# Loading layer 1's modulation weights four tiles at a time, from buffers of their own

## The chip, the cores and the metric

The kernel runs on one core of one Trainium2 chip. The metric is device time in microseconds (us) of one execution, and 2509.45 us is the median of three before the change.

## What is computed

One step of a two-layer model runs over 128 context tokens and 1024 latent tokens, each 1024 wide. Layer 0 mixes tokens by a state-space recurrence, layer 1 by windowed pooling, and each layer then has a gated feed-forward part of width 2816. In each layer six vectors, the modulation, are made from one conditioning vector per kind of token, and they shift, scale and gate everything else:

```python
def ada_mod(cond, w, b):
    m = (jax.nn.silu(cond) @ w + b)[..., None, :]
    return jnp.split(m, 6, axis=-1)

for i in range(DEPTH):
    sh1c, sc1c, g1c, sh2c, sc2c, g2c = ada_mod(c_ctx, ada_w[i], ada_b[i])
    sh1l, sc1l, g1l, sh2l, sc2l, g2l = ada_mod(c, ada_w[i], ada_b[i])
    hc, hl = modulate(xc, sh1c, sc1c), modulate(xl, sh1l, sc1l)
    ...
    xl = layer_norm(DEEPNORM_ALPHA * xl + g1l * ol, ln_g[i, 0], ln_b[i, 0])
    fl = swiglu(modulate(xl, sh2l, sc2l), ffn_w_gate[i], ffn_w_up[i], ffn_w_down[i])
    xl = layer_norm(DEEPNORM_ALPHA * xl + g2l * fl, ln_g[i, 1], ln_b[i, 1])
```

`ada_w` is 2 x 1024 x 6144 numbers of 4 bytes, so layer 1's half is 25 MB. None of layer 1's modulation is needed before layer 1 begins.

## The kernel before, in words

**The modulation in steps.** A layer's modulation is made in three banks of two vectors each. `ada_steps(l, b)` is a generator for one bank: 16 steps, each of which loads one 512 KB tile `adaw` of `ada_w` over SyncE's DMA queue (SP) and multiplies it by the conditioning (`cond`, 32 columns of which two are used) in four matmuls, one for each 32-column strip of TensorE, into one PSUM tile `ada`. In the text these four matmuls are a *group*, and groups that stand next to each other on TensorE are a *run*. After the last group the bank is finished: ScalarE copies the tile to `arow`, four small DMAs on ScalarE's queue scatter it into the 32 rows of `ar`, TensorE transposes `ar` into `adat`, and VectorE adds the bias into `mod` and derives gates (`vecs`). Before the change all of this is in the last step.

**Where the steps are taken.** `ada_rest` strings five banks together: layer 0's second and third, which are stepped in the state-space part (`ssm`), and layer 1's three. Layer 1's are taken as a filler in layer 0's feed-forward part (`build`): one step after each pass of three loops. The latent tokens are two blocks A and B of 512. `ffn_up(A)` has 22 passes, each with a gate tile and an up tile of weights and 48 matmuls `ffn` of 128x128 by 128x512. `ffn_down(A)` has 2 x 11 passes with one weight tile and 24 matmuls `dn`. `ffn_up(B)` follows, and its first four passes take the last four steps. In this stage only, `adaw` and `arow` come from the pool `raw`, three buffers of 512 KB that also take every weight tile.

**How a weight tile gets to TensorE.** SP loads it into `raw`. ScalarE rounds it to `wh`, VectorE makes the rest `wl` (`split_into`, L776 and L777), three buffers each, and TensorE multiplies `wh` twice and `wl` once (L792 to L794). The inputs of `ffn_down` are split in the same way into `hkh` and `hkl`.

**What sets the order.** Every engine and every DMA queue runs its instructions in the order in which they stand. A scheduler puts them there when the program is built, from a simulated timeline, so the order of the code is not the order on an engine.

Of the kernel before, what the change touches and what calls it, by code (L numbers as in the profile page):

```python
# [11 lines left out]
F32 = mybir.dt.float32  # L12
F32R = mybir.dt.float32r
I32 = mybir.dt.int32
AF = mybir.ActivationFunctionType
# [26 lines left out]
class Kernel:  # L42
# [88 lines left out]
    def ada_steps(self, l, b, pool=None):  # L131

        nc, I = self.nc, self.I
        def ring(n, name):
            q = pool or self.adp
            if q is None:
                return self.raw.tile([128, n], F32, tag="raw", name=name)
            return q.tile([128, n], F32, tag="ad", name=name, bufs=4 if pool else 2)

        tag = "s" if self.adp else "c"  # L140
        ps = self.psum(f"ada{l}{b}", tag)
        for hf in range(2):
            for k in range(8):
                w = ring(1024, f"adaw{l}{b}{k}{hf}")
                c0 = b * 2048 + hf * 1024
                nc.sync.dma_start(w, I["ada_w"][l, k * 128:(k + 1) * 128, c0:c0 + 1024])
                for cg in range(4):
                    nc.tensor.matmul(ps[32 * cg:32 * cg + 32, 256 * hf:256 * hf + 256], self.cond[:, k, :],
                                     w[:, cg * 256:(cg + 1) * 256], start=(k == 0), stop=(k == 7))
                if (k, hf) != (7, 1):  # L150
                    yield None
        arow = (self.raw.tile([128, 512], F32, tag="raw", name=f"arow{l}{b}") if pool
                else ring(512, f"arow{l}{b}"))
        nc.scalar.activation(arow, ps, AF.Copy)
        ar = self.sm.tile([32, 128], F32, tag="ar", name=f"ar{l}{b}", bufs=1)
        for i in range(2):
            for v in range(2):
                nc.scalar.dma_start(ar[16 * i + 8 * v:16 * i + 8 * v + 8, :], arow[i:128:32, 256 * v:256 * v + 256])
        pt = self.psum(f"adat{l}{b}", tag)
        nc.tensor.transpose(pt[:, 0:32], ar, self.ident[:32, :32])  # L160
        nc.vector.tensor_tensor(
            self.mod[l][:, 2 * b:2 * b + 2, :, :].rearrange("p v i k -> p i v k"),
            pt[:, 0:32].rearrange("p (i v k) -> p i v k", i=2, v=2),
            self.adab[:, l * 48 + b * 16:l * 48 + b * 16 + 16]
            .rearrange("p (v k) -> p v k", v=2).unsqueeze(1).to_broadcast([128, 2, 2, 8]), op=OP.add)
        self.vecs(l, b)
        yield arow

    def ada_bank(self, l, b, pool=None):
        for r in self.ada_steps(l, b, pool):  # L170
# [1 line left out]
        return r  # L172

    def ada_rest(self):
        for l, b in ((0, 1), (0, 2), (1, 0), (1, 1), (1, 2)):
            yield from self.ada_steps(l, b)


    def ssm_params(self, pool, tmp, ad):
# [459 lines left out]
    def ssm(self):  # L639
        self.adp = self.rawc = None  # L640
        R = self.side
        right, left = ExitStack(), ExitStack()
        pright = self.pright
        self.sk = left.enter_context(R("ssk", "left"))
        pp = right.enter_context(R("ssp"))
        so = right.enter_context(R("sso"))
        si = right.enter_context(R("ssi"))
        with R("sst") as tmp:
            with R("ad0", "left") as ad:
                arow = self.ssm_params(pp, tmp, ad)  # L650
            self.ssm_modvec(pp, tmp, arow)
            self.ssm_dskip(pp, tmp)
        self.u = left.enter_context(R("ssmu", "left")).tile([128, G, NCH], F32, name="u")
        self.adp = self.rawc = None
        self.Z = []
        self.late = []
        self.ada = fill = self.ada_rest()
        with R("ssu") as tmp, R("sse") as early:
            for kt in range(KT):
                self.ssm_u(tmp, kt)  # L660
                if kt == 0:
                    self.ssm_u_ctx(tmp)
                    self.Z.append(left.enter_context(R("ssmz0", "left")).tile([128, 145, 64], F32, name="Z0"))
                self.step(fill, 1)
                self.ssm_in(si, 0, kt, early, 14)
                self.ssm_tables(so, kt, si)
            while self.late:
                self.ssm_v()
        self.Z.append(left.enter_context(R("ssmz1", "left")).tile([128, 145, 64], F32, name="Z1"))
        for kt in range(KT):  # L670
            self.ssm_in(si, 1, kt, si, 3)
            self.step(fill, 1)
        while self.late:
            self.ssm_v()
        self.ssm_scan_ctx(si)
        right.close()
        pright.close()
        for t, b in (("s", 1), ("a", 5)):
            self.pp[t] = self.st.enter_context(self.tc.tile_pool(name="psx" + t, bufs=b, space=PSUM, side="right"))
        cblk = right.enter_context(R("cblk"))  # L680
        self.open_ctx(cblk)
        self.open_hc(cblk)
        with R("ssy") as tmp:
            self.adp = tmp
            self.yb = [tmp.tile([128, 8, 8, 16], F32, tag="yl", name=f"yb{q}", bufs=2) for q in range(2)]
            self.yct = [tmp.tile([128, 128], F32, name=f"yct{x}") for x in range(2)]
            for q in range(2):
                self.nc.gpsimd.memset(self.yb[q], 0.0)
                self.nc.gpsimd.memset(self.yct[q], 0.0)
            for kt in range(KT):  # L690
                self.ssm_y_ctx(tmp, kt)
                self.step(fill, 2)
            self.ctx0a()
            self.ssm_scan_lat()
            self.adp = self.rawc = None
            for kt in range(KT):
                self.ssm_y(tmp, kt)
        left.close()
        self.cright = right
# [374 lines left out]
    def build(self):  # L1074
        tc, nc = self.tc, self.nc
        with ExitStack() as st:
# [19 lines left out]
            fill = self.ctx0b()  # L1096
# [5 lines left out]
            A, B = [Block(512, 0, self.X[q], True, "a", tl, "") for q in range(2)]  # L1102
            halves = lambda b: [Block(256, 0, b.x[:, :, 256 * q:256 * q + 256], True, "a", tl, "") for q in range(2)]
            B0, B1 = halves(B)
            with tc.tile_pool(name="xm1", bufs=1) as xmp:
                xm = [xmp.tile([128, 8, 512], F32R, name=f"xm{q}") for q in range(2)]
                with tc.tile_pool(name="glup", bufs=1) as tmp:
                    xm2 = [tmp.tile([128, 8, 512], F32R, name=f"xn{q}") for q in range(2)]
                    for k in range(8):
                        yr = tmp.tile([128, 1024], F32, tag="yr", name="yr", bufs=2)  # L1110
                        nc.gpsimd.dma_start(yr, self.yd[k])
                        yv = yr.rearrange("p (t c) -> p t c", t=8)
                        tok = lambda a: a[:, k].rearrange("p (c t) -> p t c", t=8)
                        for q, x in enumerate((xm, xm2)):
                            self.split_into(tok(x[0]), tok(x[1]), yv[:, :, 64 * q:64 * q + 64])
                    self.load_x()
                    with tc.tile_pool(name="rawc", bufs=1) as self.rawc:
                        self.glu(A, xm, fill)
                        self.glu(B, xm2, fill)
                        self.drain(fill)  # L1120
                    self.rawc = None
                    self.ln(A, 0, 0, xm)
                    first = list(self.up_w(A, 0, 0))
                self.cright.close()
                hpool = tc.tile_pool(name="ffna", bufs=1, side="right")
                h = hpool.__enter__().tile([128, NF, 512], F32, name="h")
                fill = self.ada
                self.drain(self.ffn_up(A, 0, xm, h, first), fill)
                self.ln_stats(B)
                self.ln_apply(B, 0, 0, xm)  # L1130
                self.drain(self.ffn_down(A, 0, h), fill)
                self.drain(self.ffn_up(B, 0, xm, h), fill)
                self.drain(fill)
                self.ln(A, 0, 1)
            mid, side = ExitStack(), ExitStack()
            self.drain(self.ffn_down(B, 0, h))
# [10 lines left out]
            fill = self.ctx1b()  # L1147
# [9 lines left out]
            xm = [xmp.tile([128, 8, 512], F32R, name=f"xp{q}") for q in range(2)]  # L1157
            with tc.tile_pool(name="poolz", bufs=1) as tmp:
                for i, b in enumerate((A, B)):
                    for gi in range(4):  # L1160
                        w = self.pool_w(b, gi)
# [4 lines left out]
                first = list(self.up_w(A, 1, 0))  # L1166
            mid.close()
            hp = tc.tile_pool(name="ffnb", bufs=1)
            h = st.enter_context(hp).tile([128, NF, 512], F32, name="h2")
# [69 lines left out]
```

## Time and profile before

| | |
|---|---|
| median of three runs | 2509.45 us (2504.81 to 2513.17) |
| the profiled execution | 2497.54 us, span of its trace 2495.7 us |
| TensorE busy | 2293.8 us, 92% of the span |
| VectorE, ScalarE, GpSimd busy | 1280.9, 942.6, 186.0 us |
| moved by DMA | 370.56 MB, mean 148 GB/s over the span |

Shares of busy time are means over stages with different limits. Matmuls are pipelined and overlap, so the distance between the starts of two matmuls says more than their durations, and a busy share of 100% only says that TensorE was never empty. The feed-forward stage of layer 0, in which the changed steps lie, runs from about 738 us to about 1500 us of the span; the steps end at 1207 us.

### The profile page before, as it was taken

Reading aid. Unit: us, or ns where it says so; the run is one execution under the profiler, and the core shown is the slowest. Engines: PE = TensorE matmul, PEld = TensorE weight load, DVE = VectorE, ACT = ScalarE, POOL = GpSimd, SP = SyncE. Lnnn points to the kernel's source line nnn. Section 1 sums busy time; section 2 is a strip of 40 time slices with the busy share of each in tenths; the row PEclk is TensorE's granted clock in tenths of the full one; section 3 lists DMA queues with packets and bytes.
Section 4 is the critical chain, followed back from the end, with each engine's and each line's share of the span. In section 5 each row is a group of like instructions: output and inputs, shape, how many; then the busy total and the mean of one; then the engine's idle time right before and its main releaser. Section 6 shows DMA issues by size and latency. Waiting matters only on the chain.

```text
span 2495.7 us, 32988 instructions
## 1 busy us (share of the span) xinstructions
PE 2293.8 (92%) x13021; PEld 1884.2 (75%) x13021; DVE 1280.9 (51%) x2477; ACT 942.6 (38%) x1375; POOL 186.0 (7%) x190
## 2 busy tenths in 40 slices
PE   4785769899999999999999999789999999999997
PEld 2463569888887777767788888777788888888996
DVE  7578984153546222445432585778422455422476
ACT  3675216343225222433322453325322444322464
POOL 4761000000010000000000010002000100000000
PEclk8796889999999999999999999999999999999998
DMA  7767867764544435445333234875333323333463
GB/s 212 220 194 238 306 175 228 251 192 142 155 143 127 136 110 152 150 147 158 102 94 101 94 101 130 235 195 158 93 93 95 99 93 93 93 95 98 136 204 102
DMA packets 467546, 370.56 MB, mean 148 GB/s; under 512 B 20048, under 2 KB 415072, under 8 KB 465088
## 3 DMA queue, kind: packets, MB, share of 16 engines
q1 hardware_dynamic: 447600, 349.29, 46.5%
q10 hardware_dynamic: 18448, 14.58, 1.8%
q0 software_dynamic: 1344, 4.59, 0.5%
q8 instruction: 102, 1.67, 0.3%
q14 instruction: 52, 0.43, 0.1%
HBM read 345.36 MB, written 22.94 MB: 148 GB/s over the span
## 4 chain that ended last, share of the span: by engine, by line
PE 77%; DMA 5%; issue 3%; DVE 2%; ACT 1%; POOL 0%; ACTq 0%; DVEq 0%; POOLq 0%
PE ffn L792 13%; PE ffn L794 13%; PE ffn L793 13%; PE dn L792 6%; PE dn L793 6%; PE dn L794 6%; PE ffn L796 4%; PE dn L796 3%; PE glu L792 2%; PE glu L794 2%; PE glu L793 2%; PE py L630 2%; DMA raw<-ffn_w_gate 2%; DMA raw<-ffn_w_up 1%; DMA raw<-ffn_w_down 1%
## 5 line engine op out<-in xcount | busy, mean ns | idle before, releaser
L776 ACT ACTIVATE wh<-raw 128x1024 fp32r<-128x1024 f32 (+1 forms) x326 | 341.5, 1049 | 954.0 <-PE ffn L793 516.3
L777 DVE TENSOR_TENSOR wl<-raw,wh 128x1024 fp32r<-128x1024 f32 (+1 forms) x326 | 394.5, 1210 | 513.3 <-ACT wh L776 499.2
L793 PE MATMUL dn<-hkl,wh 128*128 128x512 f32 (+1 forms) x880 | 305.4, 349 | 0.0
L794 PE MATMUL dn<-hkh,wl 128*128 128x512 f32 (+1 forms) x880 | 302.8, 347 | 0.0
L792 PE MATMUL ffn<-xp,wh 128*128 128x512 f32 x704 | 277.8, 395 | 2.3 <-ACT wh L776 2.3
L794 PE MATMUL ffn<-xp,wl 128*128 128x512 f32 x704 | 279.2, 397 | 0.5 <-DVE wl L777 0.5
L793 PE MATMUL ffn<-xp,wh 128*128 128x512 f32 x704 | 279.0, 397 | 0.0
L792 PE MATMUL ffn<-xm,wh 128*128 128x512 f32 x704 | 278.1, 397 | 0.7 <-ACT xm L776 0.7
L794 PE MATMUL ffn<-xm,wl 128*128 128x512 f32 x704 | 275.1, 391 | 1.5 <-DVE wl L777 1.5
L793 PE MATMUL ffn<-xm,wh 128*128 128x512 f32 x704 | 275.6, 391 | 0.0
L792 PE MATMUL dn<-hkh,wh 128*128 128x512 f32 (+1 forms) x880 | 272.1, 351 | 0.9 <-ACT hkh L776 0.9
L837 DVE TENSOR_TENSOR h<-ffn,sg 128x512 f32<-128x512 f32 x88 | 60.6, 690 | 265.4 <-PE ffn L794 264.7
L792 PEld LDWEIGHTS dn<-hkh,wh 128*128 128x128 f32 x880 | 163.3, 190 | 30.5 <-issue 8.6
L793 PEld LDWEIGHTS dn<-hkl,wh 128*128 128x128 f32 x880 | 167.1, 190 | 22.0 <-issue 1.6
L794 PEld LDWEIGHTS dn<-hkh,wl 128*128 128x128 f32 x880 | 166.5, 189 | 21.2 <-issue 0.4
L796 PE MATMUL ffn<-xmc,raw 128*128 128x128 f32 x1184 | 147.7, 281 | 28.3 <-DMA raw<-ffn_w_gate 11.6
L796 PEld LDWEIGHTS ffn<-xmc,raw 128*128 128x128 f32 x1184 | 141.1, 195 | 37.7 <-DMA raw<-ffn_w_up 11.4
L792 PEld LDWEIGHTS ffn<-xm,wh 128*128 128x128 f32 x704 | 132.8, 189 | 37.9 <-issue 9.4
L792 PEld LDWEIGHTS ffn<-xp,wh 128*128 128x128 f32 x704 | 132.2, 188 | 35.8 <-ACT wh L776 2.5
L793 PEld LDWEIGHTS ffn<-xp,wh 128*128 128x128 f32 x704 | 132.2, 188 | 32.9 <-issue 0.7
L794 PEld LDWEIGHTS ffn<-xp,wl 128*128 128x128 f32 x704 | 132.2, 188 | 32.3 <-DVE wl L777 1.0
L794 PEld LDWEIGHTS ffn<-xm,wl 128*128 128x128 f32 x704 | 132.9, 189 | 30.5 <-DVE wl L777 1.9
(315 smaller groups left out, 3291.5 us busy)
## 6 DMA issues: line engine op xcount, KB each, us to landing
raw<-ffn_w_down SPq DMA_DIRECT2D x126, 512.0 KB
raw<-ffn_w_gate SPq DMA_DIRECT2D x125, 512.0 KB
raw<-ffn_w_up SPq DMA_DIRECT2D x125, 512.0 KB
adaw<-ada_w SPq DMA_DIRECT2D x96, 512.0 KB
raw<-ssm_glu_w SPq DMA_DIRECT2D x48, 512.0 KB
mo<-mo SPq DMA_DIRECT2D x16, 1536.0 KB
rc<-ffn_w_down SPq DMA_DIRECT2D x40, 256.0 KB
mo<-otab SPq DMA_DIRECT2D x32, 256.0 KB
```

The source lines that it names most:

```text
L630: nc.tensor.matmul(o[x], ot[:, d, x, gp, :], self.Z[d][:, d:d + NCL, 32 * x + 4 * kt + gp], start=False, stop=(d == 1))
L776: nc.scalar.activation(h, src, AF.Copy)
L777: nc.vector.tensor_tensor(l, src, h.bitcast(F32), op=OP.subtract)
L792: nc.tensor.matmul(ps, wh, xh, start=start, stop=False)
L793: nc.tensor.matmul(ps, wh, xl, start=False, stop=False)
L794: nc.tensor.matmul(ps, wl, xh, start=False, stop=stop)
L796: nc.tensor.matmul(ps, w[0], x[0], start=start, stop=stop)
L837: nc.vector.tensor_tensor(h[:, f, :], pu, sg, op=OP.mult)
```

## The change

Layer 1's modulation gets a generator of its own, `ada_late`, with a pool of its own (four buffers `ad` for weight tiles, one `arl` for `arow`) that is open during `ffn_up(A)` and `ffn_down(A)`. A step of it either issues four loads or does the 16 products of the four tiles loaded in the step before. When a bank's products are done, one more step lies between the copy with its four small DMAs and the transpose. This makes 9 steps for a bank and all three banks end within `ffn_down(A)`. For layer 0's banks `ada_steps` gets the same extra step ahead of the transpose, which is moved to `ada_end`, and `ssm` takes two more steps.

```diff
@@ ada_steps
                 nc.scalar.dma_start(ar[16 * i + 8 * v:16 * i + 8 * v + 8, :], arow[i:128:32, 256 * v:256 * v + 256])
+        yield None
+        self.ada_end(l, b, ar, tag)
+        yield arow
+
+    def ada_end(self, l, b, ar, tag):
+        nc = self.nc
         pt = self.psum(f"adat{l}{b}", tag)
         nc.tensor.transpose(pt[:, 0:32], ar, self.ident[:32, :32])
...
         self.vecs(l, b)
-        yield arow
@@ ada_rest
-        for l, b in ((0, 1), (0, 2), (1, 0), (1, 1), (1, 2)):
-            yield from self.ada_steps(l, b)
+        for b in (1, 2):
+            yield from self.ada_steps(0, b)
+
+    def ada_late(self, pool):
+
+        nc, I = self.nc, self.I
+        l = 1
+        for b in range(3):
+            ps = self.psum(f"ada{l}{b}", "c")
+            for hf in range(2):
+                for k0 in (0, 4):
+                    ws = []
+                    for k in range(k0, k0 + 4):
+                        w = pool.tile([128, 1024], F32, tag="ad", name=f"adaw{l}{b}{k}{hf}", bufs=4)
+                        c0 = b * 2048 + hf * 1024
+                        nc.sync.dma_start(w, I["ada_w"][l, k * 128:(k + 1) * 128, c0:c0 + 1024])
+                        ws.append(w)
+                    yield None
+                    for k, w in zip(range(k0, k0 + 4), ws):
+                        for cg in range(4):
+                            nc.tensor.matmul(ps[32 * cg:32 * cg + 32, 256 * hf:256 * hf + 256], self.cond[:, k, :],
+                                             w[:, cg * 256:(cg + 1) * 256], start=(k == 0), stop=(k == 7))
+                    yield None
+            arow = pool.tile([128, 512], F32, tag="arl", name=f"arow{l}{b}", bufs=1)
+            nc.scalar.activation(arow, ps, AF.Copy)
...
+            yield None
+            self.ada_end(l, b, ar, "c")
@@ ssm
                 self.step(fill, 2)
+            self.step(fill, 2)
             self.ctx0a()
@@ build
-                fill = self.ada
-                self.drain(self.ffn_up(A, 0, xm, h, first), fill)
-                self.ln_stats(B)
-                self.ln_apply(B, 0, 0, xm)
-                self.drain(self.ffn_down(A, 0, h), fill)
-                self.drain(self.ffn_up(B, 0, xm, h), fill)
-                self.drain(fill)
+                with tc.tile_pool(name="adl", bufs=1, side="right") as adl:
+                    fill = self.ada_late(adl)
+                    self.drain(self.ffn_up(A, 0, xm, h, first), fill)
+                    self.ln_stats(B)
+                    self.ln_apply(B, 0, 0, xm)
+                    self.drain(self.ffn_down(A, 0, h), fill)
+                    self.drain(fill)
+                self.drain(self.ffn_up(B, 0, xm, h))
                 self.ln(A, 0, 1)
```

**On TensorE, the products and the transpose.** Before, at the end of layer 1's first bank in `ffn_up(A)`, the last group stands behind a pass of 48 `ffn` matmuls, the transpose `adat` right behind it, and the next pass behind that:

```order
L792 MATMUL ffn_7552<-xm_4648,wh 128x512
L793 MATMUL ffn_7552<-xm_4649,wh 128x512
L794 MATMUL ffn_7552<-xm_4648,wl 128x512
L148 MATMUL ada_6550<-adaw_7616,cond 32x256 x4
L160 MATMUL adat_7629<-ident,ar_7624 128x32
L792 MATMUL ffn_7633<-xm_4648,wh 128x512
L793 MATMUL ffn_7633<-xm_4649,wh 128x512
```

In the changed program the last four groups of that bank are one run behind a pass:

```order
L829 MATMUL ffn_7025<-xm_4649,wh 128x512
L830 MATMUL ffn_7025<-xm_4648,wl 128x512
L200 MATMUL ada_6553<-adaw_7016,cond 32x256 x4
L200 MATMUL ada_6553<-adaw_7018,cond 32x256 x4
L200 MATMUL ada_6553<-adaw_7020,cond 32x256 x4
L200 MATMUL ada_6553<-adaw_7022,cond 32x256 x4
L828 MATMUL ffn_7105<-xm_4648,wh 128x512
```

The transpose of the bank now stands two whole passes, 96 matmuls, further on:

```order
L829 MATMUL ffn_7178<-xm_4649,wh 128x512
L830 MATMUL ffn_7178<-xm_4648,wl 128x512
L166 MATMUL adat_7242<-ident,ar_7172 128x32
L828 MATMUL ffn_7255<-xm_4648,wh 128x512
L829 MATMUL ffn_7255<-xm_4649,wh 128x512
```

The second bank's transpose is 96 matmuls behind its last run too, and the third's 40 `dn` matmuls behind. Counted over both lists, layer 1's 48 groups stand in 53 runs before (six groups are cut in two, two stand together) and in 17 runs now (three groups are cut).

**On SP's queue.** Before, one modulation load stands behind the gate and up loads of each pass:

```order
L785 DMA raw<-ffn_w_up 128x8x128
L146 DMA adaw_7841<-ada_w 128x1024
L785 DMA raw<-ffn_w_gate 128x8x128
L785 DMA raw<-ffn_w_up 128x8x128
L146 DMA adaw_7912<-ada_w 128x1024
L785 DMA raw<-ffn_w_gate 128x8x128
```

Now four stand together, with the weight tiles of two or three passes between such fours:

```order
L821 DMA raw<-ffn_w_gate 128x8x128
L195 DMA adaw_7247<-ada_w 128x1024
L195 DMA adaw_7249<-ada_w 128x1024
L195 DMA adaw_7251<-ada_w 128x1024
L195 DMA adaw_7253<-ada_w 128x1024
L821 DMA raw<-ffn_w_up 128x8x128
L821 DMA raw<-ffn_w_gate 128x8x128
L821 DMA raw<-ffn_w_up 128x8x128
```

A load waits for the products that last read its buffer, that is, for the run of the four before.

**On TensorE at the start of the stage.** Before, the first two groups stand there together, and the third 61 matmuls of the feed-forward part later. Now, 27 such matmuls behind the first run (tiles 6554, 6556 and a part of 6558), this stands there:

```order
L200 MATMUL ada_6553<-adaw_6558,cond 32x256 x3
L200 MATMUL ada_6553<-adaw_6560,cond 32x256 x4
L200 MATMUL ada_6553<-adaw_6708,cond 32x256 x2
...
L200 MATMUL ada_6553<-adaw_6708,cond 32x256 x2
L200 MATMUL ada_6553<-adaw_6710,cond 32x256 x4
L828 MATMUL ffn_6563<-xm_4648,wh 128x512
L829 MATMUL ffn_6563<-xm_4649,wh 128x512
L200 MATMUL ada_6553<-adaw_6712,cond 32x256 x4
L828 MATMUL ffn_6643<-xm_4648,wh 128x512
L829 MATMUL ffn_6643<-xm_4649,wh 128x512
L200 MATMUL ada_6553<-adaw_6714,cond 32x256 x4
```

The "..." stands for six `ffn` matmuls. Tiles 6712 and 6714 are loaded into the buffers of 6558 and 6560.

## Rows read from the trace of the kernel before

**Rows 1.** The page: span, and TensorE's busy time.

```profile
span 2495.7 us, 32988 instructions
...
PE 2293.8 (92%) x13021; PEld 1884.2 (75%) x13021; DVE 1280.9 (51%) x2477; ACT 942.6 (38%) x1375; POOL 186.0 (7%) x190
```

**Rows 2.** Stretches: length, busy time of each engine, TensorE's clock, DMA share, GB/s.

```profile
738.00:790.00 52.00, 49.80 (x234) 37.64 (x232) 44.78 (x59) 34.00 (x49) 7.43 (x6) 1.00 0.41 122
790.00:929.00 139.00, 139.00 (x663) 108.71 (x664) 34.76 (x34) 29.30 (x34) 0.00 (x0) 1.00 0.44 127
929.00:946.00 17.00, 12.59 (x55) 9.69 (x54) 6.53 (x9) 6.09 (x8) 0.00 (x0) 0.90 0.50 141
...
1300.00:1400.00 100.00, 100.00 (x442) 82.82 (x442) 28.28 (x27) 24.46 (x28) 0.00 (x0) 1.00 0.33 99
296.00:310.00 14.00, 11.33 (x105) 8.86 (x104) 14.00 (x85) 1.33 (x3) 0.00 (x0) 1.00 1.02 310
```

**Rows 3.** SP's timeline in `ffn_up(B)`, no steps: start, duration, issue.

```profile
1238.22 0.37 SPq L785 DMA_DIRECT2D raw<-ffn_w_gate  x1
...
1249.10 0.37 SPq L785 DMA_DIRECT2D raw<-ffn_w_gate  x1
```

**Rows 4.** TensorE's timeline, `ffn_up(A)`; x8: four matmuls, four loads of the stationary.

```profile
749.57 1.07 PE L148 MATMUL ada<-adaw,cond 128*32 128x256 f32 x16
750.57 0.50 PE L793 MATMUL ffn<-xm,wh 128*128 128x512 f32 x1
...
801.01 0.64 PE L148 MATMUL ada<-adaw,cond 128*32 128x256 f32 x8
801.58 0.50 PE L792 MATMUL ffn<-xm,wh 128*128 128x512 f32 x1
...
812.69 0.64 PE L148 MATMUL ada<-adaw,cond 128*32 128x256 f32 x8
```

**Rows 5.** TensorE's timeline where bank 0 ends; in brackets idle time and releaser.

```profile
929.49 0.64 PE L148 MATMUL ada<-adaw,cond 128*32 128x256 f32 x8
934.54 0.28 PE L160 MATMUL adat<-ident,ar 32*128 32x32 f32 x1 [4.42 <-DMA ar<-arow]
...
947.27 0.64 PE L148 MATMUL ada<-adaw,cond 128*32 128x256 f32 x8
```

**Rows 6.** The same where bank 1 ends, in `ffn_down(A)`.

```profile
1069.59 0.64 PE L148 MATMUL ada<-adaw,cond 128*32 128x256 f32 x8
1074.36 0.28 PE L160 MATMUL adat<-ident,ar 32*128 32x32 f32 x1 [4.13 <-DMA ar<-arow]
...
1082.70 0.64 PE L148 MATMUL ada<-adaw,cond 128*32 128x256 f32 x8
```

**Rows 7.** The same where bank 2 ends, in `ffn_up(B)`.

```profile
1201.67 0.64 PE L148 MATMUL ada<-adaw,cond 128*32 128x256 f32 x8
1206.75 0.24 PE L160 MATMUL adat<-ident,ar 32*128 32x32 f32 x1 [4.45 <-DMA ar<-arow]
1206.93 0.51 PE L792 MATMUL ffn<-xm,wh 128*128 128x512 f32 x1
...
1210.93 0.40 PE L794 MATMUL ffn<-xm,wl 128*128 128x512 f32 x1
```

**Rows 8.** ScalarE's timeline at the end of bank 0: the four scatters.

```profile
930.82 2.27 ACTq L158 DMA_DIRECT2D ar<-arow  x4
```

**Rows 9.** Who waited for whom, whole span: us in total, times, longest.

```profile
ACT wh L776 <- PE ffn L793: 516.3, 127, 5.7
...
SPq L785 <- DVE wl L777: 1065.1, 250, 18.1
```

**Rows 10.** The chain that ended last, context feed-forward: one weight load, issue to landing.

```profile
346.70 4.27 DMA raw<-ffn_w_gate
```

**Rows 11.** TensorE's timeline early in `ffn_up(A)`.

```profile
760.61 0.51 PE L794 MATMUL ffn<-xm,wl 128*128 128x512 f32 x1 [1.50 <-DVE wl L777]
```

**Rows 12.** VectorE's timeline in the recurrence: first context gated-linear result.

```profile
290.57 0.35 DVE L821 SCALAR_TENSOR_TENSOR sg<-glu,vv,sg 128x128 f32<-128x128 f32 x1 [3.70 <-ACT sg L820]
```

More of the change, by code (lines that the diff above doesn't have):

```diff
@@ L174, in ada_rest @@
     def ada_rest(self):
-        for l, b in ((0, 1), (0, 2), (1, 0), (1, 1), (1, 2)):
-            yield from self.ada_steps(l, b)
+        for b in (1, 2):
[21 more added lines that the diff above has]
+            nc.scalar.activation(arow, ps, AF.Copy)
+            ar = self.sm.tile([32, 128], F32, tag="ar", name=f"ar{l}{b}", bufs=1)
+            for i in range(2):
+                for v in range(2):
+                    nc.scalar.dma_start(ar[16 * i + 8 * v:16 * i + 8 * v + 8, :],
+                                        arow[i:128:32, 256 * v:256 * v + 256])
+            yield None
+            self.ada_end(l, b, ar, "c")
     def ssm_params(self, pool, tmp, ad):
@@ L656, in ssm @@
         self.late = []
-        self.ada = fill = self.ada_rest()
+        fill = self.ada_rest()
         with R("ssu") as tmp, R("sse") as early:
```

## The prediction

> **What bounds the kernel now.** I read the page first: TensorE is busy for 92% of the span [rows 1], so I looked for the stretches in which it is not, and for work on it that could be shorter. The stretches of the stage in which the changed steps lie show that TensorE is never empty in `ffn_up(A)` (139 us busy of 139) and in the part of `ffn_up(B)` that has no steps (100 of 100), while between 929 and 946 us it lacks 4.4 us and its clock falls to 0.90 [rows 2]. TensorE is the bound here, and whatever stands on it costs its full time.
>
> The timelines then give the price of each thing. A pass of 48 matmuls without a step takes 1249.10 - 1238.22 = 10.88 us, since SP issues one gate tile per pass [rows 3]; that is 0.227 us for one matmul. A pass with one group takes 812.69 - 801.01 = 11.68 us [rows 4]. A group standing alone therefore costs 0.80 us. Where two groups stand together, the matmul behind them starts 1.00 us after the run began, and behind a single group 0.57 us [rows 4]: the second group costs 0.43 us. So a run costs 0.37 us for itself and 0.43 us for each group in it.
>
> At a bank's end TensorE stands still. The transpose is behind the last group in its queue and waits for the scatter: 4.42, 4.13 and 4.45 us in the three banks [rows 5, 6, 7]. ScalarE alone needs 2.27 us to issue the four scatters [rows 8], behind its copy. What follows runs slower at first, which is the clock of 0.90 in [rows 2].
>
> **The change, part by part.** *The three stalls go.* Bank 0: from the last group to the next bank's first take 947.27 - 929.49 = 17.78 us where a pass takes 11.68, so 6.1 us are lost. Bank 1: 1082.70 - 1069.59 = 13.11 us hold two groups (1.6) and 26 matmuls (5.9), so 5.6 us are lost. Bank 2: 4.45 us of idling, and then ten distances between starts take 1210.93 - 1206.93 = 4.00 us instead of 2.27, so 6.2 us. Together **-17.9 us**. The new place of the transpose is 96 matmuls (22 us) behind the last run for two banks and 40 (9 us) for the third, and the scatter needs 934.54 - 929.49 = 5.05 us from the start of the last group, or about 6.4 us from that of a last run of four. It is hidden by those passes, and without that cover each bank would cost its 6 us again. ScalarE's copy, which waits for the run, holds up the next `wh` on its queue by the copy and the 2.27 us of scatters, but that `wh` is two tiles early. VectorE's `mod` waits for the transpose; the `wl` behind it waits for a buffer that TensorE frees at the same point, so it loses nothing.
>
> The three transposes themselves stay, now alone in the stream. No row shows one there. It takes at least the 0.2 us between it and the next start, and at most about a lone group, 0.80; as it also interrupts a stream of other matmuls, I take 0.5: **+1.5 us**.
>
> *Fewer runs.* From 53 runs with 54 whole or part groups to 17 runs with 51: 36 x 0.37 + 3 x 0.43 = **-14.6 us**. I give a part of a group the price of a whole one. No row shows a run of four at this clock; if each group kept its 0.80 us, only the three parts would be saved, 2.4 us.
>
> *SP's queue.* 48 loads leave the `raw` ring, and fours of them stand ahead of weight tiles. A four waits at the head of SP's queue until the run before has been done, about 2 us longer than the weights would have, and takes 4 x 0.35 us to issue. Its 2 MB need 7 us at the 310 GB/s that the core reaches elsewhere [rows 2]. The weight tile behind comes some 10 us later. How early is it? SP waits for `wl`, 250 times, and `wh` for TensorE, 127 times [rows 9]: a tile is issued when the one three before it has been split, which waits for TensorE to leave the tile six before. That leaves five tiles of 5.44 us, 27 us, less 4.27 us to land [rows 10] and about 2.3 us to split: 20 us to spare. Cost **0**; it becomes the rival below if the cover is gone.
>
> The Trainium skill, "DMA: Bandwidth & Descriptors", section "Queues, rings and completion order", says that each DMA engine consumes a ring's descriptors in order. By this rule the weight tile cannot overtake the four, which is the 7 us above; if it could share the bandwidth instead, it would be delayed less. By either the sum stays, as both are under the 20 us, but the rule is what makes the slower rival possible, and no row of this trace separates the two.
>
> *The start.* Tiles 6712 and 6714 cannot be loaded before the run with 6558 and 6560 is done, and their groups stand only eight matmuls and a run (3.0 us), and then two matmuls and a run, behind it. A load needs 4.27 us [rows 10], so TensorE waits 1 to 2 us for the first and under 1 us for the second. In the same place it waits 1.50 us for `wl` now [rows 11], which may hide some. I take **+2 us**, with bounds 0 and 5. Tile 6708 has 27 matmuls, 6.1 us, and is in time.
>
> *The state-space part.* Layer 0's transposes move by a step. They lie beside the recurrence on VectorE, and I find no stall at them to remove. But the results of the context's gated-linear part enter VectorE's queue at other places, the first nine recurrence steps later. It waits there 3.70 us now [rows 12], and may lose or return that much: **0**, with bounds -4 and +4.
>
> The sum is -17.9 + 1.5 - 14.6 + 2 = -29.0 us. On the profiled execution (span 2495.7, time 2497.54, 1.8 us around it) that is 2468.5 us. The median of the runs is 11.9 us longer than that execution, so I take the difference off the median: 2480.4, or **2480 us**. Nothing behind takes it back: `ffn_up(B)` is bound by TensorE again [rows 2].
>
> **Rivals.** *A group costs 0.80 us in a run of four too* (something that each change of the stationary costs). The run of two in [rows 4] speaks against it. The gain would be 17.9 + 2.4 - 1.5 - 2 = 16.8 us: 2493 us.
>
> *The first loads are late.* If each of the four runs at the start waits a whole load, 4 x 4.27 = 17 us in place of 2, the time is 2495 us. For it speaks that they depend on one another through four buffers; against it, the distances above.
>
> *Slower: the weights behind a four come too late.* The place is the `wh` of the tile behind each of the eleven later fours. It decides when the delay passes the 20 us to spare, and it makes the kernel slower by more than 0.3% when eleven times the excess passes 29 + 7.5 us, that is, from a delay of 23.3 us on. The 2 MB would have to move at about 100 GB/s (20 us, and 4 us of waiting and issuing): then 11 x 4 - 29 = 15 us slower, 2524 us. Against it speaks that the core moved 310 GB/s [rows 2]. For it: the stage moves 127 GB/s now, so a higher rate is not shown in this stage.
>
> *No change.* The gain is lost before 738 us, if the recurrence waits longer at several places; it would take seven waits like that in [rows 12]. About 2508 us.
>
> **How the numbers follow.** The forecast has 0.75; its own range is 2468 to 2490, from the bounds of the start, the recurrence and the transposes and some 4 us by which medians of three differ. The rival of the unchanged price has 0.09, the late first loads 0.06, no change 0.06, late weights 0.04. The range reaches up over the first two rivals, to 2497, and not over the last two; down it stays at 2468. About 0.3% (7.5 us) is what a measurement of this kernel can tell from no change. Faster by more than that: 0.75 + 0.09 + 0.06 = 0.90; same 0.06; slower 0.04.
>
> **What the profile would show.** Right: no idle time in front of the three transposes, clock 1.00 around them; runs of 16 matmuls of the modulation, with the next `ffn` start 1.9 us behind the run's start; passes of 10.88 us without a run and 13.0 with one. Wrong: 3.2 us more for a run of four; waits of `ada` for `adaw` of more than 5 us together, in the start or in `ffn_down(A)`; a `wh` that waits for a weight load while TensorE idles; VectorE reaching the end of the recurrence later than now by more than 4 us. A wrong sum would most likely come from the start, where several loads and runs depend on each other.

## The result

Four timed runs of the changed kernel take 2467.26 to 2476.16 us, median **2469.6 us**, against 2507.81 us before: ratio 0.985, 95% interval 0.9823 to 0.9876. In a second timing, with 17 runs of the kernel before and four of the changed one, it is 0.9869 (0.9848 to 0.989). The profiled execution takes 2467.99 us, 29.6 less than that of before. One execution of the kernel with own buffers and single groups, of 5901.44 us at a granted clock of 0.467, is left out of its ratio below.

The page of the changed kernel, answering to [rows 1]:

```profile
span 2466.2 us, 32994 instructions
...
PE 2276.6 (92%) x13021; PEld 1887.5 (77%) x13021; DVE 1279.1 (52%) x2477; ACT 941.6 (38%) x1375; POOL 187.1 (8%) x190
```

The same number of matmuls, and TensorE's share of 92% is unchanged: the share says nothing here, the stage does. Below, *the stage* is the stretch from the first to the last `ffn` matmul on `xm`. Its ends on TensorE's timeline before (start, duration, instruction):

```profile
738.42 0.62 PE L792 MATMUL ffn<-xm,wh 128*128 128x512 f32 x2
...
1404.32 0.39 PE L794 MATMUL ffn<-xm,wl 128*128 128x512 f32 x1
```

That is 665.90 us. After the change, with the places that the prediction named (idle time before an instruction and its releaser in brackets):

```profile
738.45 0.62 PE L828 MATMUL ffn<-xm,wh 128*128 128x512 f32 x2
...
757.33 1.48 PE L200 MATMUL ada<-adaw,cond 128*32 128x256 f32 x18
...
761.97 0.64 PE L200 MATMUL ada<-adaw,cond 128*32 128x256 f32 x8
763.24 0.50 PE L828 MATMUL ffn<-xm,wh 128*128 128x512 f32 x1 [0.63 <-ACT wh L812]
763.58 0.40 PE L829 MATMUL ffn<-xm,wh 128*128 128x512 f32 x1
763.90 0.64 PE L200 MATMUL ada<-adaw,cond 128*32 128x256 f32 x8
...
861.81 0.39 PE L830 MATMUL ffn<-xm,wl 128*128 128x512 f32 x1
862.13 0.24 PE L166 MATMUL adat<-ident,ar 32*128 32x32 f32 x1
862.30 0.51 PE L828 MATMUL ffn<-xm,wh 128*128 128x512 f32 x1
862.65 0.39 PE L829 MATMUL ffn<-xm,wh 128*128 128x512 f32 x1
...
873.11 0.39 PE L830 MATMUL ffn<-xm,wl 128*128 128x512 f32 x1
873.43 1.93 PE L200 MATMUL ada<-adaw,cond 128*32 128x256 f32 x32
875.30 0.50 PE L828 MATMUL ffn<-xm,wh 128*128 128x512 f32 x1
875.63 0.40 PE L829 MATMUL ffn<-xm,wh 128*128 128x512 f32 x1
875.87 0.39 PE L830 MATMUL ffn<-xm,wl 128*128 128x512 f32 x1
...
897.28 1.93 PE L200 MATMUL ada<-adaw,cond 128*32 128x256 f32 x32
...
1371.58 0.39 PE L830 MATMUL ffn<-xm,wl 128*128 128x512 f32 x1
```

The stage takes 1371.58 - 738.45 = 633.13 us, **32.8 us less**. It starts where it did (738.45 for 738.42), so nothing came from the state-space part. The first bank's transpose has no bracket: TensorE was not idle ahead of it. A run of four reaches the next matmul in 875.30 - 873.43 = 1.87 us, and two passes of which one has a run take 897.28 - 873.43 = 23.85 us, which is 10.88 + 12.97.

The 14 us around each of the three transposes after the change (length, busy time of PE, PEld, DVE, ACT, POOL, then clock, DMA share, GB/s):

```profile
857.00:871.00 14.00, 14.00 (x62) 11.29 (x62) 4.55 (x6) 3.71 (x5) 0.00 (x0) 1.00 0.26 75
964.00:978.00 14.00, 14.00 (x63) 11.29 (x62) 4.63 (x7) 3.41 (x5) 0.00 (x0) 1.00 0.27 77
1036.00:1050.00 14.00, 14.00 (x63) 11.29 (x62) 7.23 (x17) 6.30 (x10) 0.00 (x0) 1.00 0.42 132
```

TensorE is never empty there and its clock stays at the full 2.4 GHz, where [rows 2] show 0.90.

### The profile page after: what moved, and what is told of

It reads as the page before. It is cut to its first block, busy times and chain, and to the rows that moved or that the text cites. A ratio compares the mean times of both kernels' runs of the same rounds, so it can differ in the third digit from the quotient of the medians.

```text
span 2466.2 us, 32994 instructions
## 1 busy us (share of the span) xinstructions
PE 2276.6 (92%) x13021; PEld 1887.5 (77%) x13021; DVE 1279.1 (52%) x2477; ACT 941.6 (38%) x1375; POOL 187.1 (8%) x190
## 4 chain that ended last, share of the span: by engine, by line
PE 79%; DMA 10%; issue 4%; ACT 3%; DVE 3%; SPq 1%; POOL 1%; ACTq 0%; DVEq 0%; POOLq 0%
PE ffn L828 13%; PE ffn L830 13%; PE ffn L829 13%; PE dn L828 6%; PE dn L829 6%; PE dn L830 6%; PE ffn L832 4%; PE dn L832 2%; PE glu L828 2%; PE glu L830 2%; PE glu L829 2%; PE py L665 2%; DMA raw<-ffn_w_up 2%; DMA adaw<-ada_w 2%; DMA raw<-ffn_w_gate 1%
## 5 line engine op out<-in xcount | busy, mean ns | idle before, releaser
L828 PE MATMUL dn<-hkh,wh 128*128 128x512 f32 (+1 forms) x880 | 262.5, 348 | 0.8 <-ACT hkh L812 0.8
L832 PE MATMUL ffn<-xmc,raw 128*128 128x128 f32 x1184 | 148.0, 281 | 29.6 <-DMA raw<-ffn_w_gate 11.7
```

Of the source, the lines that this page charges most:

```text
L828: nc.tensor.matmul(ps, wh, xh, start=start, stop=False)
L832: nc.tensor.matmul(ps, w[0], x[0], start=start, stop=stop)
```

## The experiments

Each stands beside its stage, since the stage repeats well: the changed kernel profiled a second time has 1376.18 - 743.00 = 633.18 us, 0.05 from the first, although the 738 us ahead of it came out 4.6 us longer. In all ten profiled executions the stage begins between 733.3 and 743.0 us. This start is 4.6 of the 6.4 us by which the two of the changed kernel differ, and 2.9 of the 7.0 us between the two of before. The ratios are to the kernel before, with 95% intervals.

| kernel | transposes | runs | stage, us | ratio |
|---|---|---|---|---|
| before | behind the last group | 53 | 1404.32 - 738.42 = 665.90 | 1 |
| before, again | same | 53 | 1410.09 - 741.29 = 668.80 | 1.0002 (0.9989 to 1.0016) |
| extra step only | same | 50 | 1408.43 - 741.59 = 666.84 | 0.9991 (0.9978 to 1.0004) |
| own `arow` only | 32 to 47 matmuls later | 50 | 1385.77 - 738.84 = 646.93 | 0.9929 (0.9911 to 0.9946) |
| own buffers, singles | 36 to 48 later | 47 | 1378.42 - 733.33 = 645.09 | 0.991 (0.9891 to 0.9928) |
| twos | 40 to 96 later | 33 | 1380.82 - 739.56 = 641.26 | 0.9898 (0.9882 to 0.9915) |
| changed, again | 40 to 96 later | 17 | 1376.18 - 743.00 = 633.18 | 0.9869 (0.9848 to 0.989) |
| loads on GpSimd's queue | 40 to 96 later | 17 | 1370.19 - 738.64 = 631.55 | 0.9868 (0.9853 to 0.9883) |
| whole array | 40 to 96 later | 16 | 1426.30 - 738.70 = 687.60 | 1.0083 (1.0063 to 1.0103) |

**Which edit takes the stalls away.** The change brings two things that could: the extra step and a buffer of its own for the copied row. First the buffer alone, in the kernel before:

```diff
         arow = (self.raw.tile([128, 512], F32, tag="raw", name=f"arow{l}{b}") if pool
+                else self.adl.tile([128, 512], F32, tag="arl", name=f"arow{l}{b}", bufs=1) if l == 1
                 else ring(512, f"arow{l}{b}"))
...
+                with tc.tile_pool(name="adl", bufs=1, side="right") as self.adl:
```

> The kernel before with one edit: in layer 1's banks the copied row `arow` has a buffer of its own and no longer takes one of the ring `raw`. By the order, the transposes then stand 41, 32 and 47 matmuls behind their last groups; the groups stay single (50 runs, 52 parts). Theory of the sum (stalls and runs are separate prices): the three stalls go (-17.9 us), three lone transposes stay (+1.3, as the changed kernel's trace shows 0.42 us each), three runs and two parts less (-1.9): 18.5 us less than before, a profiled execution near 2479 us, ratio near 0.9926. Rival (the buffers for the weight tiles and the fours carry the whole gain): within 3 us of before, ratio 0.999 or more.

Measured: 0.9929, and the stage 19.0 us shorter. TensorE's timeline at the first bank's transpose in this kernel:

```profile
939.97 0.24 PE L161 MATMUL adat<-ident,ar 32*128 32x32 f32 x1
940.14 0.51 PE L795 MATMUL ffn<-xm,wl 128*128 128x512 f32 x1
```

No idle time. Then the extra step alone:

```diff
+        yield None
         pt = self.psum(f"adat{l}{b}", tag)
         nc.tensor.transpose(pt[:, 0:32], ar, self.ident[:32, :32])
...
                 self.step(fill, 2)
+            self.step(fill, 2)
             self.ctx0a()
```

> The kernel before with the extra step ahead of each transpose, in both layers, and nothing else: `arow` and the weight tiles stay in `raw`. By the order, layer 1's three transposes still stand right behind their last groups. Theory of the sum: the stalls stay, three runs and three parts less give -2.4 us: near 2495 us, ratio near 0.999. Rival (the extra step is what takes the stalls away): 2479 us, ratio near 0.993.

Measured: 0.9991, no change that can be told from none. The same place on TensorE's timeline, in this kernel:

```profile
937.64 0.28 PE L161 MATMUL adat<-ident,ar 32*128 32x32 f32 x1 [4.37 <-DMA ar<-arow]
937.85 0.80 PE L794 MATMUL ffn<-xm,wh 128*128 128x512 f32 x1
938.45 0.63 PE L795 MATMUL ffn<-xm,wh 128*128 128x512 f32 x1
938.87 0.63 PE L794 MATMUL ffn<-xm,wh 128*128 128x512 f32 x1
```

The stall is there as before, with distances of 0.42 us behind it in place of 0.227, the lower level of the clock (its mean in the 14 us around the stall is 0.76). So the step that reads like the fix does not move the transpose, which the scheduler places; the small buffer does. Why the scheduler puts the transpose behind passes once `arow` leaves the ring was not measured. It would fit that a row in `raw` keeps a weight tile out, so that there is no other work to put ahead of the transpose, but that is an argument only: a row in the ring beside runs of four was not tried on the chip.

**What a run costs.** The changed kernel's buffers with one group per step (47 runs), and with two (33 runs):

```diff
+            if l == 1:
+                return self.adl.tile([128, n], F32, tag="ad", name=name, bufs=4)
             if q is None:
                 return self.raw.tile([128, n], F32, tag="raw", name=name)
```

(in the kernel before, beside `arow`'s buffer and the extra step for layer 1's banks), and

```diff
                     for k, w in zip(range(k0, k0 + 4), ws):
+                        if k == k0 + 2:
+                            yield None
                         for cg in range(4):
```

in the changed one.

> The kernel before with four buffers for layer 1's weight tiles, one for `arow` and the extra step, but one group per step: 47 runs in place of the changed kernel's 17. By the order, the transposes stand 48, 36 and 48 matmuls behind their last groups. Theory of the sum: the stalls go as in the changed kernel, and the 30 more runs and two more parts cost 30 x 0.37 + 2 x 0.43 = 12.0 us: near 2480 us on a profiled execution, ratio to before near 0.993. Rival (a run has no price of its own, the buffers carry the gain): near 2468 us, as the changed kernel.

> The changed kernel with two groups per step in place of four: 33 runs in place of 17, 58 whole or cut groups in place of 51. Theory of the sum: the stage from the first `ffn` on `xm` to the last, 633.1 us in the changed kernel, takes 16 x 0.37 = 5.9 us more, and up to 7 x 0.43 = 3.0 us more for the cuts: 639 to 642 us, the time near 2476 us. Rival (a run has no price of its own): 633 us.

Measured: 645.09 and 641.26 us, 11.9 and 8.1 us over the changed kernel's 633.18, where 12.0 and 5.9 to 8.9 were expected. The rival, 633 us, is out. With equal buffers and no stalls the time follows the number of runs.

**What the 0.37 us of a run is.** Four tiles of `cond` as a stationary of 128 columns, so that the modulation runs on the whole array as the feed-forward part does (the values of layer 1's modulation are left out, since every product reads the same four tiles):

```diff
-                            nc.tensor.matmul(ps[32 * cg:32 * cg + 32, 256 * hf:256 * hf + 256], self.cond[:, k, :],
-                                             w[:, cg * 256:(cg + 1) * 256], start=(k == 0), stop=(k == 7))
+                            nc.tensor.matmul(ps[:, 256 * hf:256 * hf + 256], self.cond[:, 0:4, :],
+                                             w[:, cg * 256:(cg + 1) * 256], start=(k + cg == 0), stop=(k + cg == 10))
```

> The changed kernel with each matmul of layer 1's modulation on the whole array: the stationary has 128 columns (four tiles of `cond`) in place of 32, and the four no longer lie side by side in column strips. Layer 1's modulation is then not the reference's; the rest is. What is asked is why a run costs 0.37 us beside its groups. If it is the change from strips to the whole array and back, a run of sixteen now costs sixteen matmuls and next to nothing beside them (under 0.1 us). If it is another thing (the change of number format, the drain of the pipeline), 0.3 to 0.4 us stay. The matmuls themselves should take 4 x 0.43 us per group, so that the stage is about 48 x 1.29 = 62 us longer than 633 us; by the first theory 6 us less than that.

Measured: the stage 54.5 us longer, where the first theory said 56. TensorE's timeline at one run of sixteen:

```profile
975.51 0.40 PE L830 MATMUL ffn<-xm,wl 128*128 128x512 f32 x1
975.74 7.07 PE L200 MATMUL ada<-adaw,cond 128*128 128x256 f32 x32
982.46 0.58 PE L828 MATMUL ffn<-xm,wh 128*128 128x512 f32 x1
982.88 0.40 PE L829 MATMUL ffn<-xm,wh 128*128 128x512 f32 x1
983.12 0.39 PE L830 MATMUL ffn<-xm,wl 128*128 128x512 f32 x1
...
1049.63 1.89 PE L200 MATMUL ada<-adaw,cond 128*128 128x256 f32 x8
1051.17 0.58 PE L828 MATMUL dn<-hkh,wh 128*128 128x512 f32 x1
```

A run of 16 reaches the next matmul in 6.72 us and one of four in 1.54, so one such matmul costs 5.18 / 12 = 0.43 us. From the matmul ahead of the run to the third behind it 983.12 - 975.51 = 7.61 us pass; less three matmuls (0.68) and 16 x 0.43 (6.91), 0.0 is left. The same sum for the strips, 875.87 - 873.11 = 2.76 us less 0.68 and 4 x 0.43, leaves 0.36. So the price of a run goes away when its matmuls use the whole array, in the same number format: it is that of going from the whole array to column strips and back. The Trainium skill, "TensorEngine Tiling (Array Packing)", section "Tiling Modes", says that a change of the tiling mode drains TensorE; the two traces agree so far as they show the price, 0.36 us for there and back in this stream, and not the drain itself.

**Whether fours on SP's queue cost anything.** The 48 loads on GpSimd's queue:

```diff
-                        nc.sync.dma_start(w, I["ada_w"][l, k * 128:(k + 1) * 128, c0:c0 + 1024])
+                        nc.gpsimd.dma_start(w, I["ada_w"][l, k * 128:(k + 1) * 128, c0:c0 + 1024])
```

> The changed kernel with layer 1's 48 loads issued on GpSimd's queue instead of SP's: SP has only the weight tiles again. Theory (the fours on SP's queue cost nothing): the stage takes 633 us, within 1.5 us. Rival (the fours hold up weight tiles, and TensorE pays for it somewhere): more than 3 us less, 630 us or below.

Measured: 631.55 us, 1.6 us less than the changed kernel, between the two bounds; the timed ratio is the same. Two cut groups fewer account for up to 0.9 us of it, and the wait of 0.63 us at 763.24 us, which this kernel does not have, for the rest. As shown below, that wait does not come from a late weight tile, and SP issues the gate tile at 762.53 us here for 763.09 there. So these rows show no cost of the fours; TensorE's order at the start of the stage differs between the two kernels.

**What a stall costs from one execution to the next.** The kernel before, profiled again, with no edit:

> The kernel before, profiled once more. In its first trace layer 0's feed-forward stage, from the first `ffn` on `xm` to the last, took 665.9 us, and the clock was 0.88 in the 14 us around each stall; in the run with the extra step, which has the same stalls, it was 0.76, and each stall cost about 1.4 us more. Theory 1 (the price of a stall differs from execution to execution): the stage takes 665.9 us or up to some 670, with a clock between 0.76 and 0.88 at the stalls. Theory 2 (the dearer stalls come from the extra step): 665.9 us and 0.88 again.

The 14 us around the stalls, first in the first trace of before, then in this one:

```profile
930.00:944.00 14.00, 9.59 (x39) 7.73 (x36) 4.97 (x8) 5.53 (x8) 0.00 (x0) 0.88 0.52 153
1069.00:1083.00 14.00, 9.87 (x54) 6.46 (x53) 5.82 (x10) 5.25 (x7) 0.00 (x0) 0.88 0.57 187
1202.00:1216.00 14.00, 9.55 (x42) 7.41 (x35) 5.15 (x11) 5.09 (x6) 0.00 (x0) 0.88 0.66 185
```

```profile
933.00:947.00 14.00, 9.46 (x29) 7.55 (x30) 4.83 (x8) 4.89 (x7) 0.00 (x0) 0.76 0.54 153
1074.00:1088.00 14.00, 9.87 (x48) 6.77 (x51) 5.10 (x9) 4.67 (x6) 0.00 (x0) 0.76 0.48 157
1207.00:1221.00 14.00, 9.57 (x38) 7.35 (x33) 4.97 (x10) 4.32 (x5) 0.00 (x0) 0.76 0.66 180
```

The same idle time, 4.1 to 4.6 us, but a lower mean clock at all three stalls, and a stage 2.9 us longer. Theory 1 holds: the price of a stall is not one number. The trace on which the prediction stood showed the cheap case. Beside this second trace, whose clock of 0.76 it shares, the stage of the kernel with the extra step is 2.0 us shorter, near the 2.4 us that its fewer runs and parts were expected to give.

## Why the prediction held, step by step

**Right: the bound and the three stalls.** TensorE set the stage's time, and what was taken off it came back in full. The buffer for `arow` alone gave 19.0 us where 18.5 were expected. A lone transpose costs 0.39 us (862.65 - 861.81 = 0.84 less two matmuls of 0.227); 0.5 was taken.

**Right: fewer runs, -14.6 us.** A run of four reaches the next matmul in 1.87 us (1.9 forecast), and undoing the packing costs 11.9 us for 30 runs (12.0 expected). The rival that each group keeps its 0.80 us is out.

**Mis-sized: the start, +2 us.** The loads there were in time. I had counted from the wrong instruction: a load waits for the products of its own buffer, and those of tile 6558 are the first in the run at 757.33, not its end. That leaves 761.97 - 757.33 = 4.6 us for the load in place of 3.0, and TensorE is not idle ahead of that group. What TensorE did wait for, 0.63 us at 763.24, is a `wh`. It was not late for want of a weight tile, as the slower rival has it, but by its place on ScalarE, which was not idle ahead of it: a table load and `sg` stand there. The one wait of a `wh` for a load in the stage comes over 7 us later, and TensorE is not idle then. ScalarE's timeline after the change:

```profile
760.35 1.28 ACT L872 ACT_TABLE_LOAD   x1
761.65 0.60 ACT L872 ACTIVATE sg<-ffn 128x512 f32<-128x512 f32 x1
762.14 2.00 ACT L812 ACTIVATE wh<-raw 128x1024 fp32r<-128x1024 f32 x2
...
770.96 1.06 ACT L812 ACTIVATE wh<-raw 128x1024 fp32r<-128x1024 f32 x1 [0.73 <-DMA raw<-ffn_w_gate]
```

The kernel before has that wait for a load too, and a longer one:

```profile
768.94 1.06 ACT L776 ACTIVATE wh<-raw 128x1024 fp32r<-128x1024 f32 x1 [1.03 <-DMA raw<-ffn_w_gate]
```

Where before TensorE was idle for 2.18 us at this point of the stage (1.50 for `wl`, 0.68 for `xm`), it is now for 1.28 (0.65 for `xm`, 0.63 for `wh`). The term is -0.9 and not +2, which is most of the 3.8 us between the stage's -32.8 and the sum's -29.0.

**Right: SP's queue later, 0.** Behind 770.96 us no `wh` of the stage waits for a load, and another queue brings nothing that these rows show. How far the 20 us of spare time would have reached was not tried.

**Right: the state-space part, 0.** The stage starts 0.03 us later in the first of the changed kernel's traces than in the first of before. Executions of one kernel differ there by up to 4.6 us, so a change smaller than that is not shown. The extra step, which moves layer 0's transposes too, is worth nothing on its own.

**Wrong: that nothing behind takes it back.** From the end of the stage to the last `dn` before takes 2469.48 - 1404.32 = 1065.16 us, after 2439.75 - 1371.58 = 1068.17. These 3.0 us are lost ahead of 1751 us, in layer 1's first part; from there on the two traces run in step. The other traces have 1065.9 and 1066.0 with the stalls, and 1067.7 to 1073.1 without. Of the 3.0 us, 2.2 are lost by the `pst` matmuls (1774.63 us before, 1744.13 now), and I found no cause for them: the context's feed-forward part there waits for its loads one by one, and the places of a few VectorE and ScalarE instructions differ, but no run separates these. The other 0.8 us go with the clock. Right behind `pst` TensorE is idle for 2.26 us in all ten traces. After it the clock stays at 1.00 in the two traces of before and is lower in the eight others, here the first of before and of the changed kernel (columns as above):

```profile
1777.90:1781.10 3.20, 2.64 (x10) 1.90 (x11) 2.36 (x2) 0.92 (x1) 0.00 (x0) 1.00 0.35 121
```

```profile
1747.40:1750.60 3.20, 3.13 (x7) 2.03 (x8) 2.36 (x2) 0.92 (x1) 0.00 (x0) 0.50 0.34 122
```

The profiled execution came out at 2467.99 us against 2468.5 by luck: this loss and the gain at the start cancelled.

**Mis-sized: from the profiled execution to the median.** I took the 11.9 us between the profile of before and its median for an offset that stays. The changed kernel's first median lies 1.6 us above its profile. Part of the offset may belong to the stalls: the second trace of before, 7.0 us longer than the first, has 2.9 us of this in the stage, at the lower clock, and these go with the stalls. Another 2.9 us lie ahead of the stage, where executions of one kernel differ. The timed runs have no traces, so where their offset lies is not shown. The median fell by 38 us in the first timing and by 35 in the second, and came out near the lower end of the range.

## What to carry to other kernels

Where TensorE is the bound, take the price of each thing on it from distances between starts, and count pieces in the order that was built: here the sum then held to 3.8 us in the stage. Ask of a stall which resource put the waiting instruction there; here 2 KB per partition outside a shared ring gave over half of the gain (19.0 of 32.8 us), and the extra step by itself gave nothing. Matmuls in column strips amid work on the whole array are cheaper in a few long runs than in many short ones.

## What was not expected of the hardware

An idle time of 4.1 to 4.6 us on TensorE was followed by matmuls 0.43 us apart, the lower clock level, at every stall, and for a length that differed between executions of one program: a mean clock of 0.88 in 14 us in one, 0.76 in another, alike at all three stalls of an execution. An idle time of 2.26 us in layer 1, the same in ten traces, left the clock at 1.00 behind it in two of them and not in eight. Going to column strips and back costs 0.36 us, while the change between these matmuls and the feed-forward part's, both on the whole array, costs nothing that these rows show.
